# Layer 0's output product with 512 columns throughout, and its first feed-forward pair from the scaled residual stream

## Chip, cores and metric

One core of a Trainium2 chip runs the whole kernel in one launch. The metric is the device time of that launch in microseconds (us), taken as the median of repeated runs. The engines are named as in the profile: PE (TensorE, matrix products; PEld loads its stationary operand), DVE (VectorE), ACT (ScalarE), POOL (GpSimd) and SP (SyncE, which issues the DMAs).

## What is computed

Two layers of a diffusion trunk on 512 tokens of width 1024: 256 latent tokens x and 256 context tokens ctx, which go through the same weights with modulation values of their own. Layer 1 computes the latent tokens alone behind its attention. What matters here is the seam of layer 0 between the output product and the feed-forward network, for both halves of the tokens:

```python
def rms_norm(x, g):
    y = x * lax.rsqrt(jnp.mean(x * x, axis=-1, keepdims=True) + EPS)
    return y * g

m = ga * (ya @ w_br_a) + gb * (yb @ w_br_b) + gc * (yc @ w_br_c)
x = x + gx1 * (m @ w_out)                       # output product, 1024 x 1024
u2 = rms_norm(x, norm2_g) * (1 + cx2) + sx2     # scale cx2, shift sx2
x = x + gx2 * ((silu(u2 @ w_ff1) * (u2 @ w_ff3)) @ w_ff2)   # 1024 -> 2816 -> 1024
```

The modulation values (sx2, cx2 and the others) are six products of a conditioning vector with a 1024 x 6144 matrix in each layer; the ctx half has its own.

## The kernel before

**Products.** All data stand with the features on the 128 partitions and the tokens in the free dimension. Numbers are fp32. Weights and activations are split into a high and a low part, and each product is three matmuls (`mm3`, L227 to L229): high by high, high weight by low activation, low weight by high activation. A weight unit is 256 rows by 256 columns; one DMA on SP brings it as `raw`, one ACT copy makes its high part `wh` (L133) and one DVE subtraction its low part `wl` (L145). Both work ahead of PE by a few units; seven `raw` buffers stand ready, so that the next DMA waits for the `wl` that frees one. Results are accumulated in four PSUM banks (`acc`), two for each pair of 128 output columns.

**The stretch.** `into_job` makes 256 output columns of `w_out` in a job; jp counts the four jobs. `into` sets up jp 0 and 1 with all 512 tokens, then jp 2 and 3 for the x half with 256 tokens and again for the ctx half; the second run uses the weight parts of the first. For each 128 output columns DVE adds the product times a gate to the residual stream, once for each half (`xT`, L1135), and ACT and DVE square it and sum the squares (`ssq`, L530). At jp 3 of a half, `norm_rest` is put to the side work: one product with ones sums the squares over the partitions (`ss`, L543), ACT and DVE make the reciprocal root (`rstd`, `norm_rstd`), and `norm_u` goes over the eight blocks of 128 features: `ut` = x times scale times rstd (DVE, L571), `uh` = ut plus shift (ACT), `ul` = the rest (DVE, L580). The first feed-forward pair (`ff_job` with fp 0: 256 columns of `w_ff1` and 256 of `w_ff3`) then runs on the x half and, with the same weight parts, on the ctx half. The other ten pairs run with 512 tokens.

**What sets the order.** Each engine runs its instructions in the order in which the program puts them; a scheduler behind the program's text may move one a few places. The main loop goes over the jobs and after every few matmuls lets the side generators take a step. One generator, `mod_bg`, makes modulation groups in the background: for group j it loads eight pieces of 512 KB (`mraw`, two buffers, issued on SP among the `raw`), and for each piece and each half DVE multiplies and adds 1024 columns (`macc`, L489 and L491); then come two transposes (L496), two reduces (L497), a small product (L501) and four additions into `mod` (L505). In this stretch group 8 (shift and scale of the feed-forward norm) ends and group 10 runs. `hold`, set at jp 3 with the norm and cleared at the end of `norm_u`, stops this generator.

**Layer 1** runs its own first pair already in another way (`ff_first`, L1302 to L1304): the operand is x times the scale, split into `xh` (ACT) and `xl` (DVE, L1283) by `scaled_u`, with the shift as two more columns of `xh` (so 258 columns). The norm and the shift are put in behind the products: `ff` = product times rstd (L1310), `b` = the sum of the two shift columns (L1312), then silu with `b` as bias.

Of the kernel before, what the change touches and what calls it, by code (L numbers as in the profile page):

```python
# [8 lines left out]
F32 = mybir.dt.float32  # L9
# [5 lines left out]
P = 128  # L15
D = 1024
KT = D // P
SEQ = 256
# [156 lines left out]
class Trunk:  # L175
    def __init__(self, ctx, tc, a, out):
        self.nc, self.tc, self.a, self.out = tc.nc, tc, a, out
        self.cp = ctx.enter_context(tc.tile_pool(name="cp", bufs=1))
        self.gp = ctx.enter_context(tc.tile_pool(name="gp", bufs=61))
# [12 lines left out]
        self.xr = []  # L192
        self.keep = deque()
        self.plain = {}
# [337 lines left out]
    def norm_open(self, l, which):  # L532
        self.r0 = self.g([P, TOK], name="rstd")
        self.which = l, which
        last = self.which == (DEPTH - 1, 1)
        self.uu = [self.gT(SEQ, "u") if last else self.g2([P, TOK], "u") for _ in range(KT)]

    def norm_rstd(self, c):

# [19 lines left out]
    def norm_u(self, kts, vs):  # L559

        nc = self.nc
        l, which = self.which
        todo = [(kt, slice(v * SEQ, (v + 1) * SEQ), v) for kt in kts for v in vs]
        ts = {}

        def normed(i):
            if i < len(todo):
                kt, c, v = todo[i]
                ts[i] = self.g([P, SEQ], name="ut")
                g = self.A[l][which][:, kt, v : v + 1]  # L570
# [4 lines left out]
        for i, (kt, c, v) in enumerate(todo):  # L575
            hi, lo = (t[:, c] for t in self.uu[kt])
# [646 lines left out]
    def into_job(self, l, name, g0, which, sl, jp, k0=0, nkt=KT, more=False):  # L1223

        w = self.a[name][l]
        norm = jp == 3 and not more
        plain = which == 0 and l == DEPTH - 1

        def run(get):
            rhs = self.m if which == 0 else self.h[k0 : k0 + nkt]  # L1230
# [36 lines left out]

    def split_shift(self, l):

        t = self.sp.tile([P, KT, 2], F32R, tag="sh", bufs=1, name="shift")  # L1270
        sh = self.mod[l][:, 24 : 24 + KT, 0]
        self.split(t[:, :, 0], t[:, :, 1], sh)
# [12 lines left out]

    def ff_first(self, l):


        def run(get):
            nc = self.nc  # L1290
            mm = nc.tensor.matmul
            res = []
            for i in range(2):
                ps = [self.acc(), self.acc()]
                for u in range(KT // 2):
                    hi, lo = get(256)
                    for c in range(2):
                        cs = slice(c * P, (c + 1) * P)
                        for k in range(2):
                            kt = 2 * u + k  # L1300
                            xh, xl = self.plain[kt]
                            mm(ps[c][:, : SEQ + 2], hi[:, k, cs], xh, start=kt == 0, stop=False)  # L1302
                            mm(ps[c][:, :SEQ], hi[:, k, cs], xl, start=False, stop=False)
                            mm(ps[c][:, : SEQ + 2], lo[:, k, cs], xh, start=False, stop=kt == KT - 1)  # L1304
                        yield
                self.side.until(lambda: "rstd" in self.done)
                for c in range(2):
                    b = self.small(1, "b")
                    t = self.g([P, SEQ], name="ff")
                    nc.vector.tensor_tensor(t, ps[c][:, :SEQ], self.r0[:, :SEQ], ALU.mult)  # L1310
                    nc.scalar.activation(b, ps[c][:, SEQ : SEQ + 1], AF.Copy)
                    nc.vector.tensor_tensor(b, b, ps[c][:, SEQ + 1 : SEQ + 2], ALU.add)  # L1312
                    if i == 0:
                        nc.scalar.activation(t, t, AF.Silu, bias=b)
                        res.append(t)
                        continue
                    nc.vector.scalar_tensor_tensor(t, t, b, res[c], ALU.add, ALU.mult)
                    h = self.gT(SEQ, "h")
                    self.split(h[0], h[1], t)
                    self.h.append(h)  # L1320

        return self.units(self.a["w_ff1"][l], 0) + self.units(self.a["w_ff3"][l], 0), run

    def norm_rest(self, sl, ends):
        yield NORM_C if sl.start else NORM_X
        self.norm_rstd(sl)
        if self.which == (DEPTH - 1, 1):
            self.done.add("rstd")
# [127 lines left out]
    def program(self):  # L1456
        jobs = []
        self.bg_jobs = [(0, j, 2) for j in range(4, 12, 2)] + [(1, j, 2 if j < 4 else 1) for j in range(0, 12, 2)]
        for l in range(DEPTH):
# [17 lines left out]
            whole = slice(0, T)  # L1477
            parts = [slice(v * SEQ, (v + 1) * SEQ) for v in range(T // SEQ)]

            def into(*args):  # L1480

                res = [self.into_job(*args[:4], whole, jp, *args[4:]) for jp in range(2)]
                return res + [self.into_job(*args[:4], sl, jp, *args[4:]) for sl in parts for jp in range(2, 4)]

            jobs += into(l, "w_out", 16, 0)
            for f0, f1 in ((0, FT),) if last else ((0, FFA), (FFA, FT)):
                for fp in range(f0 // 2, f1 // 2):
                    if fp == 0 and last:
                        jobs.append(self.ff_first(l))
                        continue  # L1490
                    jobs += [self.ff_job(l, sl, fp) for sl in (parts if fp == 0 else [whole])]
                if last:
                    need = {("mod", l, 10), ("mod", l, 11)}

# [7 lines left out]
                elif f1 < FT:  # L1502
                    jobs += [self.into_job(l, "w_ff2", 40, 1, whole, jp, f0, f1 - f0, True) for jp in range(4)]
                else:
                    jobs += into(l, "w_ff2", 40, 1, f0, f1 - f0)
        return jobs

    def run(self):
# [75 lines left out]
```

## Time and profile before

| | before |
|---|---|
| time, median of 3 runs | 1229.56 us (1229.47 to 1229.62) |
| profiled execution | 1229.05 us, its span 1227.2 us |
| PE busy | 1196.7 us (98%) |
| DVE busy | 928.7 us (76%) |
| ACT busy | 643.2 us (52%) |
| DMA, mean over the span | 151 GB/s |

Times in rows are microseconds from the start of the span. A duration is longer than the distance to the next start where instructions overlap in an engine's pipeline, so costs are taken from starts. A tile's name is that of the program without its number, and L1135 is line 1135 of the kernel. A row's bracket gives the time for which the engine was idle before it, and what it waited for.

### The profile page before, as it was taken

Reading aid. Unit: us, or ns where it says so; the run is one execution under the profiler, and the core shown is the slowest. Engines: PE = TensorE matmul, PEld = TensorE weight load, DVE = VectorE, ACT = ScalarE, POOL = GpSimd, SP = SyncE. Lnnn points to the kernel's source line nnn. Section 1 sums busy time; section 2 is a strip of 40 time slices with the busy share of each in tenths; the row PEclk is TensorE's granted clock in tenths of the full one; section 3 lists DMA queues with packets and bytes.
Section 4 is the critical chain, followed back from the end, with each engine's and each line's share of the span. In section 5 each row is a group of like instructions: output and inputs, shape, how many; then the busy total and the mean of one; then the engine's idle time right before and its main releaser. Section 6 shows DMA issues by size and latency. Waiting matters only on the chain.

```text
span 1227.2 us, 20247 instructions
## 1 busy us (share of the span) xinstructions
PE 1196.7 (98%) x7059; PEld 1059.1 (86%) x7059; DVE 928.7 (76%) x1744; ACT 643.2 (52%) x1393; POOL 136.6 (11%) x185
## 2 busy tenths in 40 slices
PE   7899999999999999999999999998999999999998
PEld 2788889788888988888888888998999999999987
DVE  5867789989898996768566764778889778765554
ACT  4755587666434543332223333456878667655642
POOL 3243410101100000000000000154012100000000
PEclk9899999999999999999999999999999999999999
DMA  8722244334464535455666663243244565666563
GB/s 288 217 78 76 76 134 123 98 104 158 129 207 144 173 104 180 154 165 162 197 201 195 206 203 114 79 126 92 83 115 115 154 195 167 197 183 182 162 194 114
DMA packets 157522, 185.44 MB, mean 151 GB/s; under 512 B 12792, under 2 KB 135532, under 8 KB 157420
## 3 DMA queue, kind: packets, MB, share of 16 engines
q1 hardware_dynamic: 155612, 181.49, 47.6%
q0 software_dynamic: 1808, 2.66, 1.9%
q8 instruction: 55, 0.90, 0.3%
q14 instruction: 47, 0.39, 0.1%
HBM read 183.05 MB, written 1.05 MB: 150 GB/s over the span
## 4 chain that ended last, share of the span: by engine, by line
PE 80%; DVE 6%; DMA 5%; ACT 3%; POOL 3%; issue 2%; SPq 1%; DVEq 0%; ACTq 0%; POOLq 0%
PE acc L227 24%; PE acc L228 24%; PE acc L229 24%; DMA whole<-in_w_mod_dram 2%; PE y L842 2%; DMA raw<-in_w_in_dram 1%; DVE wl L145 1%; PE pt L888 1%; PE s L865 1%; POOL rs L686 1%; ACT wh L133 1%; PE s L866 1%; DVE macc L491 1%; ACT p L831 1%; DMA mraw<-in_w_mod_dram 1%
## 5 line engine op out<-in xcount | busy, mean ns | idle before, releaser
L133 ACT ACTIVATE wh<-raw 128x512 fp32r<-128x512 f32 (+2 forms) x512 | 307.9, 613 | 361.3 <-PE acc L228 229.7
L145 DVE TENSOR_TENSOR wl<-raw,wh 128x512 fp32r<-128x512 f32 (+2 forms) x512 | 343.3, 679 | 151.4 <-ACT wh L133 148.0
L227 PE MATMUL acc<-uh,wh 128*128 128x512 f32 (+1 forms) x784 | 279.8, 358 | 2.1 <-DVE v L239 1.0
L229 PE MATMUL acc<-uh,wl 128*128 128x512 f32 (+1 forms) x784 | 277.4, 355 | 2.4 <-DVE wl L145 2.4
L228 PE MATMUL acc<-ul,wh 128*128 128x512 f32 (+1 forms) x784 | 277.9, 355 | 0.2 <-DVE ul L580 0.2
L491 DVE SCALAR_TENSOR_TENSOR macc<-mraw,sf,macc 128x1024 f32<-128x1024 f32 x112 | 144.6, 1295 | 49.0 <-DMA mraw<-in_w_mod_dram 48.8
L229 PEld LDWEIGHTS acc<-uh,wl 128*128 128x128 f32 x784 | 148.9, 190 | 22.8 <-DVE wl L145 2.6
L227 PEld LDWEIGHTS acc<-uh,wh 128*128 128x128 f32 x784 | 148.7, 190 | 22.8 <-ACT gate L1100 1.8
L228 PEld LDWEIGHTS acc<-ul,wh 128*128 128x128 f32 x784 | 149.1, 190 | 19.9 <-DVE ul L580 0.4
L227 PE MATMUL acc<-wh,uh 128*128 128x384 f32 (+1 forms) x304 | 100.4, 331 | 4.6 <-ACT uh L1376 4.4
L228 PE MATMUL acc<-wl,uh 128*128 128x384 f32 (+1 forms) x304 | 98.8, 325 | 2.3 <-DVE wl L145 2.3
L229 PE MATMUL acc<-wh,ul 128*128 128x384 f32 (+1 forms) x304 | 99.0, 326 | 0.0
L227 PE MATMUL acc<-u,wh 128*128 128x256 f32 x320 | 91.4, 286 | 0.1
L229 PE MATMUL acc<-u,wl 128*128 128x256 f32 x320 | 91.0, 284 | 0.0
L228 PE MATMUL acc<-u,wh 128*128 128x256 f32 x320 | 90.5, 283 | 0.0
L227 PE MATMUL acc<-hh,wh 128*128 128x512 f32 (+1 forms) x216 | 75.9, 351 | 0.0
L229 PE MATMUL acc<-hh,wl 128*128 128x512 f32 (+1 forms) x216 | 75.6, 350 | 0.0
L228 PE MATMUL acc<-hl,wh 128*128 128x512 f32 (+1 forms) x216 | 75.5, 350 | 0.0
L227 PEld LDWEIGHTS acc<-wh,uh 128*128 128x128 f32 x304 | 59.2, 195 | 6.1 <-ACT uh L1376 4.5
L228 PEld LDWEIGHTS acc<-wl,uh 128*128 128x128 f32 x304 | 59.5, 196 | 3.5 <-DVE wl L145 2.6
L227 PEld LDWEIGHTS acc<-u,wh 128*128 128x128 f32 x320 | 61.4, 192 | 0.8 <-issue 0.5
L229 PEld LDWEIGHTS acc<-u,wl 128*128 128x128 f32 x320 | 61.4, 192 | 0.3 <-issue 0.2
(287 smaller groups left out, 2326.8 us busy)
## 6 DMA issues: line engine op xcount, KB each, us to landing
raw<-in_w_ff_dram SPq DMA_DIRECT2D x264, 256.0 KB, 3.0
mraw<-in_w_mod_dram SPq DMA_DIRECT2D x80, 512.0 KB, 4.0
raw<-in_w_in_dram SPq DMA_DIRECT2D x112, 256.0 KB, 2.9
raw<-in_w_in_dram SPq DMA_DIRECT2D x144, 64.0 KB, 2.0
whole<-in_w_mod_dram SPq DMA_DIRECT2D x32, 256.0 KB, 5.1
raw<-in_w_out_dram SPq DMA_DIRECT2D x32, 256.0 KB, 2.9
raw<-in_w_in_dram SPq DMA_DIRECT2D x16, 192.0 KB, 3.2
raw<-in_w_br_c_dram SPq DMA_DIRECT2D x8, 256.0 KB, 3.0
```

The source lines that it names most:

```text
L133: self.nc.scalar.activation(hi[:, :n], self.raw[i][:, :n], AF.Copy)
L145: self.nc.vector.tensor_tensor(lo[:, :n], self.raw[i][:, :n], self.hi[i][:, :n].bitcast(F32), ALU.subtract)
L227: mm(out, st[0], mv[0], start=start, stop=False)
L228: mm(out, st[0], mv[1], start=False, stop=False)
L229: mm(out, st[1], mv[0], start=False, stop=stop)
L491: nc.vector.scalar_tensor_tensor(acc[v], w, c, acc[v], ALU.mult, ALU.add)
L686: nc.gpsimd.tensor_tensor(rs, rs, self.mhalf[:, : 4 * nh], ALU.pow)
L831: nc.scalar.activation(pt, ps, AF.Exp, scale=-1.0, bias=m, accum_out=s[:, 0:1])
L842: mm(o, st, t[:, kt % 2, :], start=kt == 0 and i == 0, stop=kt == n - 1 and i == 1)
L865: nc.tensor.matmul(ps, st, ks[h][0], start=True, stop=False)
L866: nc.tensor.matmul(ps, st, ks[h][1], start=False, stop=True)
L888: nc.tensor.transpose(ps[:, kt * P : (kt + 1) * P], pr[h, qt][:, kt * P : (kt + 1) * P], self.ident)
```

## The change

Layer 0 runs all four jobs of `w_out` with 512 tokens (`into([whole], ...)`), and its first feed-forward pair becomes `ff_first`, which so far only layer 1 used. `ff_first` now takes the number of halves `nv` from the tokens: for `w_ff1` it runs the x half and then the ctx half with the same weight parts, and so for `w_ff3`. `scaled_u` splits x times scale for each half. So `plain` holds in both layers, and group 8 of the modulation must be done by jp 0 of `w_out`. `norm_rest` runs once for 512 tokens and tells with `("rstd", l)` that the evacuation may begin. `u` is still made for the pairs from 1 on; its tiles are taken one by one in `norm_u`, and the pool `gp` has 60 buffers of a slightly larger size where it had 61. Lines of the new code stand 1 to 10 higher (L1135 is L1136, L571 is L570, L580 is L581, L1283 is L1287, L1310 and L1312 are L1320 and L1322).

```diff
     def scaled_u(self, l, kt):
...
-        hi, lo = self.g([P, SEQ + 2], F32R, name="xh"), self.g([P, SEQ], F32R, name="xl")
-        x, g = self.xT[:, kt, 0:SEQ], self.A[l][1][:, kt, 0:1]
-        nc.scalar.activation(hi[:, :SEQ], x, AF.Copy, scale=g)
-        nc.scalar.activation(hi[:, SEQ:], self.shift[:, kt, :].bitcast(F32), AF.Copy)
-        nc.vector.scalar_tensor_tensor(lo, x, g, hi[:, :SEQ].bitcast(F32), ALU.mult, ALU.subtract)
+        nv = self.T // SEQ
+        hi = self.g([P, nv, SEQ + 2], F32R, name="xh")
+        lo = self.g([P, nv, SEQ], F32R, name="xl")
+        for v in range(nv):
+            x, g = self.xT[:, kt, v * SEQ : (v + 1) * SEQ], self.A[l][1][:, kt, v : v + 1]
+            nc.scalar.activation(hi[:, v, :SEQ], x, AF.Copy, scale=g)
+            nc.vector.scalar_tensor_tensor(lo[:, v, :], x, g, hi[:, v, :SEQ].bitcast(F32), ALU.mult, ALU.subtract)
+        nc.scalar.activation(hi[:, :, SEQ:], self.shift[:, kt, 0:nv, :].bitcast(F32), AF.Copy)
...
     def ff_first(self, l):
+        nv = self.tokens // SEQ
...
             for i in range(2):
-                ps = [self.acc(), self.acc()]
-                for u in range(KT // 2):
-                    hi, lo = get(256)
+                us = []
+                for v in range(nv):
+                    ps = [self.acc(), self.acc()]
+                    for u in range(KT // 2):
+                        if v == 0:
+                            us.append(get(256))
+                        hi, lo = us[u]
...
+                                mm(ps[c][:, : SEQ + 2], hi[:, k, cs], xh, start=kt == 0, stop=False)
+                                mm(ps[c][:, :SEQ], hi[:, k, cs], xl, start=False, stop=False)
+                                mm(ps[c][:, : SEQ + 2], lo[:, k, cs], xh, start=False, stop=kt == KT - 1)
+                            yield
+                    self.side.until(lambda: ("rstd", l) in self.done)
                     for c in range(2):
...
+                        nc.vector.tensor_tensor(t, ps[c][:, :SEQ], self.r0[:, v * SEQ : (v + 1) * SEQ], ALU.mult)
+                        nc.scalar.activation(b, ps[c][:, SEQ : SEQ + 1], AF.Copy)
+                        nc.vector.tensor_tensor(b, b, ps[c][:, SEQ + 1 : SEQ + 2], ALU.add)
...
-            jobs += into(l, "w_out", 16, 0)
+            jobs += into([whole], l, "w_out", 16, 0)
             for f0, f1 in ((0, FT),) if last else ((0, FFA), (FFA, FT)):
                 for fp in range(f0 // 2, f1 // 2):
-                    if fp == 0 and last:
-                        jobs.append(self.ff_first(l))
-                        continue
-                    jobs += [self.ff_job(l, sl, fp) for sl in (parts if fp == 0 else [whole])]
+                    jobs.append(self.ff_job(l, whole, fp) if fp else self.ff_first(l))
```

**How the order moves.** The rows below are instructions in the order in which an engine runs them, with the program's numbers on the tiles; they carry no times.

DVE at the end of the first output job. `acc_715` and `acc_716` are its accumulators, `mraw0_10_k` piece k of group 10. Before:

```order
L242 SCALAR_TENSOR_TENSOR ml_714_4493<-mix_712_4489,mh_713_4492 128x512
L145 TENSOR_TENSOR wl147_4552<-raw147_4405,wh147_4538 128x512
L1135 SCALAR_TENSOR_TENSOR xT_83<-acc_715_4496,mod0_110,xT_83 128x256 x2
L1135 SCALAR_TENSOR_TENSOR xT_83<-acc_716_4497,mod0_110,xT_83 128x256 x2
L505 TENSOR_TENSOR mod0_110<-modt_719_4578,cols0_109 32x16 x4
L145 TENSOR_TENSOR wl_724_4592<-raw148_4427,wh_717_4556 128x512
L530 TENSOR_TENSOR ssq_84<-ssq_84,sq_718_4575 128x512
L520 SCALAR_TENSOR_TENSOR A01_112<-mod0_110,cols0_109 128x16
L145 TENSOR_TENSOR wl_726_4611<-raw149_4454,wh_725_4596 128x512
L491 SCALAR_TENSOR_TENSOR macc_720_4585<-mraw0_10_1_4587,sf_105,macc_720_4585 128x1024
```

The same place after:

```order
L491 SCALAR_TENSOR_TENSOR macc_719_4506<-mraw0_10_1_4507,sf_105,macc_719_4506 128x1024
L242 SCALAR_TENSOR_TENSOR ml_714_4493<-mix_712_4489,mh_713_4492 128x512
L145 TENSOR_TENSOR wl147_4572<-raw147_4405,wh147_4557 128x512
L491 SCALAR_TENSOR_TENSOR macc_718_4505<-mraw0_10_2_4550,sf_105,macc_718_4505 128x1024
L1136 SCALAR_TENSOR_TENSOR xT_83<-acc_715_4496,mod0_110,xT_83 128x256 x2
L145 TENSOR_TENSOR wl148_4617<-raw148_4427,wh148_4576 128x512
L1287 SCALAR_TENSOR_TENSOR xl_721_4588<-xT_83,A01_112,xh_720_4587 128x256
L1136 SCALAR_TENSOR_TENSOR xT_83<-acc_716_4497,mod0_110,xT_83 128x256
L1287 SCALAR_TENSOR_TENSOR xl_721_4588<-xT_83,A01_112,xh_720_4587 128x256
L1136 SCALAR_TENSOR_TENSOR xT_83<-acc_716_4497,mod0_110,xT_83 128x256
L491 SCALAR_TENSOR_TENSOR macc_719_4506<-mraw0_10_2_4550,sf_105,macc_719_4506 128x1024
```

The four additions L505 and the gain L520, which stood behind the first residuals, now stand ahead of them (with `mix_709` and `mix_712`, just above these rows); three `macc` have come ahead too, and each residual is followed by an `xl`.

DVE at the norm. Before, in the norm of the ctx half; `wl_811` is the low part of the last unit of `w_ff3`, and `acc_814` and `acc_815` belong to the first pair:

```order
L580 SCALAR_TENSOR_TENSOR ul_760_4857<-ut_807_5091,mod0_110,uh_759_4856 128x256
L571 SCALAR_TENSOR_TENSOR ut_810_5106<-xT_83,A01_112,rstd_758_4855 128x256
L580 SCALAR_TENSOR_TENSOR ul_762_4859<-ut_808_5093,mod0_110,uh_761_4858 128x256
L145 TENSOR_TENSOR wl_811_5109<-raw163_4777,wh_803_5074 128x512
L571 SCALAR_TENSOR_TENSOR ut_812_5123<-xT_83,A01_112,rstd_758_4855 128x256
L580 SCALAR_TENSOR_TENSOR ul_764_4861<-ut_809_5096,mod0_110,uh_763_4860 128x256
L580 SCALAR_TENSOR_TENSOR ul_766_4863<-ut_810_5106,mod0_110,uh_765_4862 128x256
L491 SCALAR_TENSOR_TENSOR macc_720_4585<-mraw0_10_6_5234,sf_105,macc_720_4585 128x1024
L571 SCALAR_TENSOR_TENSOR ut_813_5134<-xT_83,A01_112,rstd_758_4855 128x256
L571 SCALAR_TENSOR_TENSOR ut_816_5152<-xT_83,A01_112,rstd_758_4855 128x256
L580 SCALAR_TENSOR_TENSOR ul_768_4865<-ut_812_5123,mod0_110,uh_767_4864 128x256
```

After, in the norm of both halves; `acc_761` and `acc_762` are the accumulators of the group w1 by x half, `acc_785` and `acc_786` those of w1 by ctx half:

```order
L581 SCALAR_TENSOR_TENSOR ul_780_5021<-ut_776_4995,mod0_110,uh_779_5020 128x256
L570 SCALAR_TENSOR_TENSOR ut_782_5033<-xT_83,A01_112,rstd_758_4926 128x256
L581 SCALAR_TENSOR_TENSOR ul_780_5021<-ut_777_5005,mod0_110,uh_779_5020 128x256
L1320 TENSOR_TENSOR ff_759_4927<-acc_761_4929,rstd_758_4926 128x256
L1320 TENSOR_TENSOR ff_760_4928<-acc_762_4930,rstd_758_4926 128x256
L570 SCALAR_TENSOR_TENSOR ut_789_5057<-xT_83,A01_112,rstd_758_4926 128x256
L1322 TENSOR_TENSOR b_783_5036<-b_783_5036,acc_761_4929 128x1
L581 SCALAR_TENSOR_TENSOR ul_788_5055<-ut_781_5023,mod0_110,uh_787_5054 128x256
L1322 TENSOR_TENSOR b_784_5041<-b_784_5041,acc_762_4930 128x1
L570 SCALAR_TENSOR_TENSOR ut_790_5067<-xT_83,A01_112,rstd_758_4926 128x256
L581 SCALAR_TENSOR_TENSOR ul_788_5055<-ut_782_5033,mod0_110,uh_787_5054 128x256
L1320 TENSOR_TENSOR ff_759_4927<-acc_785_5046,rstd_758_4926 128x256
```

Before, the low part of the last unit and the second norm stood here, and four `macc` of group 10 after. Now `ut` and `ul` of both halves, a transpose and a reduce of group 10 (just above and below these rows) stand around the evacuation of the first pair.

PE at the first pair. Before, the products of the ctx half with `w_ff3` read the normalised `uh` and `ul`:

```order
L227 MATMUL acc_815_5138<-uh_767_4864,wh_801_5056 128x256
L228 MATMUL acc_815_5138<-ul_768_4865,wh_801_5056 128x256
L229 MATMUL acc_815_5138<-uh_767_4864,wl_802_5070 128x256
L227 MATMUL acc_815_5138<-uh_769_4866,wh_801_5056 128x256
L228 MATMUL acc_815_5138<-ul_770_4867,wh_801_5056 128x256
L229 MATMUL acc_815_5138<-uh_769_4866,wl_802_5070 128x256
```

After, where the third group (w3 by x half, `acc_805`) follows the second (w1 by ctx half, `acc_786`):

```order
L1312 MATMUL acc_786_5047<-xh_756_4918,wh_749_4870 128x258
L1313 MATMUL acc_786_5047<-xl_757_4919,wh_749_4870 128x256
L1314 MATMUL acc_786_5047<-xh_756_4918,wl_750_4884 128x258
L1312 MATMUL acc_805_5146<-xh_720_4587,wh_751_4888 128x258
L1313 MATMUL acc_805_5146<-xl_721_4588,wh_751_4888 128x256
L1314 MATMUL acc_805_5146<-xh_720_4587,wl_763_4931 128x258
L1312 MATMUL acc_805_5146<-xh_723_4604,wh_751_4888 128x258
```

The operands are now `xh` and `xl`, and `acc_805` uses the PSUM bank that `acc_761` had, `acc_806` that of `acc_762`, and the fourth group (`acc_821`, `acc_822`) those of `acc_785` and `acc_786`. Pair 1 follows with the banks of the third group.

## Rows read from the trace of the kernel before

**Rows 1.** The page: busy time (us, share, instructions) of PE; the chain by engine.
```profile
PE 1196.7 (98%) x7059; PEld 1059.1 (86%) x7059; DVE 928.7 (76%) x1744; ACT 643.2 (52%) x1393; POOL 136.6 (11%) x185
...
PE 80%; DVE 6%; DMA 5%; ACT 3%; POOL 3%; issue 2%; SPq 1%; DVEq 0%; ACTq 0%; POOLq 0%
```

**Rows 2.** Timeline of PE: start us, duration, line, tiles, [idle before <-releaser].
```profile
380.79 0.39 PE L227 MATMUL acc<-mh,wh 128*128 128x512 f32 x1
...
402.79 0.28 PE L227 MATMUL acc<-mh,wh 128*128 128x256 f32 x1
...
441.07 0.38 PE L229 MATMUL acc<-uh,wl 128*128 128x256 f32 x1 [2.41 <-DVE wl L145]
...
442.52 0.41 PE L229 MATMUL acc<-uh,wl 128*128 128x256 f32 x1
...
444.65 0.34 PE L227 MATMUL acc<-uh,wh 128*128 128x256 f32 x1
...
445.54 0.28 PE L228 MATMUL acc<-ul,wh 128*128 128x256 f32 x1
...
455.14 0.40 PE L227 MATMUL acc<-uh,wh 128*128 128x512 f32 x1
```

**Rows 3.** Slices: us, busy PE, PEld, DVE, ACT, POOL, then clock, DMA share, GB/s.
```profile
400.00:413.00 13.00, 13.00 (x100) 12.49 (x99) 12.76 (x19) 6.02 (x11) 0.00 (x0) 1.00 0.62 197
413.00:426.00 13.00, 13.00 (x107) 12.74 (x106) 12.75 (x24) 7.57 (x16) 0.00 (x0) 1.00 0.55 168
426.00:440.00 14.00, 12.51 (x96) 11.71 (x94) 13.70 (x34) 8.45 (x20) 0.00 (x0) 1.00 0.40 118
440.00:455.00 15.00, 13.93 (x103) 13.93 (x104) 13.78 (x24) 5.78 (x12) 0.00 (x0) 0.89 0.35 119
455.00:470.00 15.00, 15.00 (x70) 12.47 (x69) 8.39 (x13) 4.97 (x9) 0.00 (x0) 1.00 0.34 106
```

**Rows 4.** Timeline of DVE from the start of the output product.
```profile
380.34 0.68 DVE L1115 SCALAR_TENSOR_TENSOR mix<-gate,acc 128x512 f32<-128x512 f32 x1
380.93 0.68 DVE L145 TENSOR_TENSOR wl<-raw,wh 128x512 fp32r<-128x512 f32 x1
...
390.51 0.88 DVE L1135 SCALAR_TENSOR_TENSOR xT<-acc,mod,xT 128x256 f32<-128x256 f32 x2 [2.59 <-PE acc L229]
...
392.67 0.71 DVE L505 TENSOR_TENSOR mod<-modt,cols 32x16 f32<-32x16 f32 x4
...
399.69 2.48 DVE L491 SCALAR_TENSOR_TENSOR macc<-mraw,sf,macc 128x1024 f32<-128x1024 f32 x2 [0.70 <-DMA mraw<-in_w_mod_dram]
402.19 1.68 DVE L1135 SCALAR_TENSOR_TENSOR xT<-acc,mod,xT 128x256 f32<-128x256 f32 x4
...
440.33 0.69 DVE L145 TENSOR_TENSOR wl<-raw,wh 128x512 fp32r<-128x512 f32 x1
```

**Rows 5.** Timeline of PE in layer 1's first pair; 29 steps lie between.
```profile
1031.78 0.28 PE L1302 MATMUL acc<-xh,wh 128*128 128x258 f32 x1
...
1035.27 0.28 PE L1304 MATMUL acc<-xh,wl 128*128 128x258 f32 x1
```

**Rows 6.** Timeline of DVE behind the first pair: a transpose.
```profile
451.01 1.24 DVE L496 STREAM_TRANSPOSE mtr<-macc 128x1024 f32<-128x1024 f32 x1
```

**Rows 7.** Timeline of DVE in layer 1: evacuation of the first pair.
```profile
1042.43 0.75 DVE L1310 TENSOR_TENSOR ff<-acc,rstd 128x256 f32<-128x256 f32 x2
```

**Rows 8.** What DVE waited for from 380 to 426 us: total, times, longest.
```profile
DVE xT L1135 <- PE acc L229: 3.1, 2, 2.6
DVE macc L491 <- DMA mraw<-in_w_mod_dram: 0.9, 2, 0.7
DVE ml L242 <- ACT mh L237: 0.7, 1, 0.7
DVE wl L145 <- ACT wh L133: 0.6, 2, 0.3
```

**Rows 9.** The page: a DMA issue's KB and us to landing.
```profile
mraw<-in_w_mod_dram SPq DMA_DIRECT2D x80, 512.0 KB, 4.0
```

More of the change, by code (lines that the diff above doesn't have):

```diff
@@ L178, in __init__ @@
         self.cp = ctx.enter_context(tc.tile_pool(name="cp", bufs=1))
-        self.gp = ctx.enter_context(tc.tile_pool(name="gp", bufs=61))
+        self.gp = ctx.enter_context(tc.tile_pool(name="gp", bufs=60))
         self.wp = ctx.enter_context(tc.tile_pool(name="wp", bufs=4))
@@ L534, in norm_open @@
         self.which = l, which
-        last = self.which == (DEPTH - 1, 1)
-        self.uu = [self.gT(SEQ, "u") if last else self.g2([P, TOK], "u") for _ in range(KT)]
+        self.uu = [None if l or which else self.g2([P, TOK], "u") for _ in range(KT)]
     def norm_rstd(self, c):
@@ L575, in norm_u @@
         for i, (kt, c, v) in enumerate(todo):
+            if self.uu[kt] is None:
+                self.uu[kt] = self.gT(SEQ, "u") if self.which == (DEPTH - 1, 1) else self.g2([P, TOK], "u")
             hi, lo = (t[:, c] for t in self.uu[kt])
@@ L1226, in into_job @@
         norm = jp == 3 and not more
-        plain = which == 0 and l == DEPTH - 1
+        plain = which == 0
         def run(get):
@@ L1268, in split_shift @@
     def split_shift(self, l):
-        t = self.sp.tile([P, KT, 2], F32R, tag="sh", bufs=1, name="shift")
-        sh = self.mod[l][:, 24 : 24 + KT, 0]
-        self.split(t[:, :, 0], t[:, :, 1], sh)
+        nv = self.T // SEQ
+        t = self.sp.tile([P, KT, 2, 2], F32R, tag="sh", bufs=1, name="shift")
+        sh = self.mod[l][:, 24 : 24 + KT, 0:nv]
+        self.split(t[:, :, 0:nv, 0], t[:, :, 0:nv, 1], sh)
         self.flush()
@@ L1278, in scaled_u @@
         nc = self.nc
[L1279 to L1283 removed]
+        nv = self.T // SEQ
+        hi = self.g([P, nv, SEQ + 2], F32R, name="xh")
[5 more added lines that the diff above has]
+        nc.scalar.activation(hi[:, :, SEQ:], self.shift[:, kt, 0:nv, :].bitcast(F32), AF.Copy)
         self.plain[kt] = hi, lo
     def ff_first(self, l):
+        nv = self.tokens // SEQ
         def run(get):
@@ L1291, in run @@
             mm = nc.tensor.matmul
-            res = []
+            res = [self.g([P, nv, SEQ], name="ff") for _ in range(2)]
             for i in range(2):
-                ps = [self.acc(), self.acc()]
-                for u in range(KT // 2):
-                    hi, lo = get(256)
-                    for c in range(2):
[L1298 to L1315, printed above, removed]
-                        continue
[L1317 to L1320, printed above, removed]
@@ L1322, in ff_first @@
-        return self.units(self.a["w_ff1"][l], 0) + self.units(self.a["w_ff3"][l], 0), run
+                us = []
[5 more added lines that the diff above has]
+                        hi, lo = us[u]
+                        for c in range(2):
+                            cs = slice(c * P, (c + 1) * P)
+                            for k in range(2):
+                                kt = 2 * u + k
+                                xh, xl = (x[:, v, :] for x in self.plain[kt])
+                                mm(ps[c][:, : SEQ + 2], hi[:, k, cs], xh, start=kt == 0, stop=False)
[3 more added lines that the diff above has]
+                    self.side.until(lambda: ("rstd", l) in self.done)
+                    for c in range(2):
+                        b = self.small(1, "b")
+                        t = res[c][:, v, :] if i == 0 else self.g([P, SEQ], name="ff")
+                        nc.vector.tensor_tensor(t, ps[c][:, :SEQ], self.r0[:, v * SEQ : (v + 1) * SEQ], ALU.mult)
+                        nc.scalar.activation(b, ps[c][:, SEQ : SEQ + 1], AF.Copy)
+                        nc.vector.tensor_tensor(b, b, ps[c][:, SEQ + 1 : SEQ + 2], ALU.add)
+                        if i == 0:
+                            nc.scalar.activation(t, t, AF.Silu, bias=b)
+                            continue
+                        nc.vector.scalar_tensor_tensor(t, t, b, res[c][:, v, :], ALU.add, ALU.mult)
+                        if v == 0:
+                            self.h.append(self.gT(self.T, "h"))
+                        self.split(*(x[:, v * SEQ : (v + 1) * SEQ] for x in self.h[c]), t)
@@ L1324, in norm_rest @@
+        keep = ("keep",) if nv > 1 else ()
+        return [u + keep for u in self.units(self.a["w_ff1"][l], 0) + self.units(self.a["w_ff3"][l], 0)], run
     def norm_rest(self, sl, ends):
@@ L1326, in norm_rest @@
         self.norm_rstd(sl)
-        if self.which == (DEPTH - 1, 1):
-            self.done.add("rstd")
+        if self.which[1]:
+            self.done.add(("rstd", self.which[0]))
         vs = range(sl.start // SEQ, sl.stop // SEQ)
@@ L1504, in program @@
                 else:
-                    jobs += into(l, "w_ff2", 40, 1, f0, f1 - f0)
+                    jobs += into(parts, l, "w_ff2", 40, 1, f0, f1 - f0)
         return jobs
```

3 lines of the change are left out of this document (1 added, 2 removed).

## Prediction

> **What bounds the kernel now.** I read the totals first: PE is busy for 98% of the span and carries 80% of the chain that ended last [rows 1]. By that alone any PE time saved would be time saved. The change, however, sits in one stretch, from the first matmul of layer 0's output product at 380.79 to the first full-width feed-forward matmul of column pair 1 at 455.14 [rows 2], 74.35 us. So I read that stretch by slices [rows 3]: from 400 on VectorE (DVE, the third of the busy figures) is busy for 12.76 of 13, 12.75 of 13, 13.70 of 14 and 13.78 of 15 us, while PE loses time only in the last two slices. Here two engines are full together, and PE is barely ahead. Where PE does lose time it loses it to DVE: 2.41 us before 441.07, waiting for a `wl` of L145 [rows 2, 4].
>
> What PE has to do there: a matmul with 512 columns takes 0.227 us from start to start (380.79 to 402.79 is 96 of them and a small one), one with 256 takes 0.12 (80 from 445.54 to 455.14) [rows 2]. So 96 x 0.227 + 384 x 0.12 + about 0.9 for the sums of squares = 68.8 us; the other 5.6 are the 2.41, a stretch at half clock behind it (10 matmuls from 442.52 to 444.65 at 0.213 instead of 0.12, about 17 in all, so 1.6 us) and small gaps [rows 2].
>
> **What the change takes from PE.** Of the output product 192 matmuls of 256 become 96 of 512: 23.0 to 21.8 us. The first pair's 192 stay at 256 or 258 columns; layer 1 runs that form already at 3.49 us for 29 steps, 0.120 each [rows 5]. New PE work: 192 x 0.227 + 192 x 0.120 + 0.9 = 67.5 us, and 0.3 for the small products, 67.8. Had PE nothing to wait for, pair 1 would start at 380.79 + 67.8 = 448.6, 6.5 us before 455.14: 1.2 of narrow matmuls and 5.3 of present loss, because the products no longer wait for normalised values.
>
> **What it puts on DVE.** Per 256 columns of each of 16 blocks there is one `xl` (L1287 of the new code): 16 x 0.40 = 6.3 us, at the pitch of the residual's four in a row (1.68 us for four of 0.48, so 0.40 each) [rows 4]. The 16 `ut` and 16 `ul` of the norm stay, since the pairs from 1 on still read normalised values. The evacuation of the first pair gains sixteen instructions, eight of them with one column, and the sums of squares lose some: small. More important is order. In the old code the norm of the x half set `hold` before the background product of modulation group 10 was done; its last four `macc` (0_10_6, 0_10_7) stood behind the whole norm, under the easy slice that follows. The new code sets `hold` only at the last of the four blocks, so all 14 `macc` still open, and their two transposes, now stand before or within the norm. And PE now needs two things of DVE that come late in that order. There are four accumulators; the third group of the first pair (w3, x half) takes the banks that the first group (w1, x half) gives back when `b_784` is added, and the fourth (w3, ctx half) those that `b_804` gives back.
>
> So the time is a sum over DVE's queue. Start at `mix_709<-gate` (380.34 [rows 4]), which stands at the same point in both orders, and count to the end of `b_784`: 110 instructions. 40 with 512 columns (24 of them `wl`) x 0.60 (380.34 to 380.93 [rows 4]) = 24.0; 14 `macc` x 1.20 (two in 2.48, of which the second lasts 1.28 [rows 4]) = 16.8; 16 residuals and 16 `xl` x 0.395 = 12.6; 7 `ut` and 5 `ul` = 4.7; two transposes and a reduce of 1024 at about 1.15 (a transpose lasts 1.24, less the 0.08 by which neighbours overlap [rows 4, 6]) = 3.5; two evacuations x 0.335 (0.75 for two of 0.42 [rows 7]) = 0.7; modulation adds (four in 0.71 [rows 4]) and the smallest rows = 1.0. Sum 63.3: **not before 443.6**, even if DVE never idles. PE, by its own work, reaches that point at 380.79 + 43.5 + 11.5 + 0.9 + 0.3 = 437.0.
>
> How much idle comes on top? The same sum over the old order, 102 instructions from the same start to the `wl` at 440.33, is 53.8 against 60.6 passed [rows 4, 6], 6.8 of idle: 3.1 for PE, 0.9 for transfers, 0.7 and 0.6 for ScalarE [rows 8], the rest gaps. The 3.1 goes: those residuals waited from 387.9 to 390.51 [rows 4], and now three `macc` and the four adds, 4.4 us, stand ahead of them. ScalarE's 1.3 and the gaps of 1.5 I leave. Transfers: the loads of 0_10_4 and 0_10_6 are queued on SP behind `raw156` and `raw160`, which wait for a `wl` five or six rows before the `macc` that reads them: 4.0 us of flight [rows 9], after the issue of the `raw` ahead, against 4.2 to 4.4 us of DVE work between, so about 0.5 each. Some of these waits will cover others. I take 2.5, from bounds of 0 (nothing but the queue) and 5 (all of the old idle but PE's, with both transfers as long again).
>
> - w3 x half starts at 443.6 + 2.5 = 446.1, some nine us after PE could have.
> - From `b_784` to `b_804` are 7.5 us of DVE work (fourteen `ut` and `ul`, a reduce, two evacuations, two `b`). That gives 453.6. The third group's 5.8 us on PE, and 1.6 more if the clock falls as it did after 441.07, lie inside it.
> - w3 ctx half 453.6 + 5.8 = 459.4. Pair 1 takes the banks that `b_817` frees, 5.4 us after `b_804` (six `ut` and `ul`, two `wl`, four adds of group 10, two evacuations with their `b` and one product), 459.0, so it isn't late again. Its start: 459.5, **4.4 us later than 455.14**; I add 0.3 for restarts of PE.
>
> Nothing is given back after: in 455 to 470 PE is busy for 15.00 of 15 with DVE at 8.39 [rows 3]; that the `macc` are done earlier only empties a slice that was not full. The profiled run (1229.05, span 1227.2) becomes 1233.8; against the median of 1229.56 the same +4.7 gives **1234.3**.
>
> **A rule against the row.** DVE is full in four slices in a row and PE is not [rows 3]. The Trainium skill (Perfetto Trace Analysis, "Identifying the Most-Contended Engine" and "Optimization Strategy") says to improve the engine with the highest occupancy, with the reservation that the most-contended engine may change between regimes. By the first half the PE work removed would come off the time: 448.6 for pair 1 and 1223 in all, the first rival below; the second half is what the slices show.
>
> **The rivals.**
>
> *PE sets the end (faster, 1223.1).* DVE reaches `b_784` before PE does, since the products wait for no normalised values: pair 1 at 448.6, 6.5 us earlier. For it: totals [rows 1], and layer 1, where the same form ran without a wait [rows 5]. Against it: layer 1 has 256 tokens, so half the `xl`, `ut` and `ul`, and no `macc` in between; the 63.3 us of work ahead of `b_784` would have to be 54.
>
> *DVE's queue without idle (no change, 1231.5).* If idle is 0, w3 x half starts at 443.6, w3 ctx half at 451.1 and pair 1 at 457.0 with the restarts: +1.9. For it: slices with 12.76 of 13 [rows 3]. Against it: 1.3 us of waits for ScalarE that the change doesn't remove [rows 8], and more work on ScalarE (16 `xh`).
>
> *Longer waits and a second fall of the clock (slower, 1238).* Idle of 5 gives 448.6, 456.1 for w3 ctx half; if PE then runs that group's first part at half clock, as it did from 441.07 to 444.65 after 2.41 us of waiting (steps of 0.213, the 1.2 GHz level; granted clock 0.89 over the slice [rows 2, 3]), 1.6 more: 456.1 + 5.8 + 1.6 = 463.5, +8.4. It decides if PE waits in the fourth group as it does in the third. Beside the row: the Trainium skill (TensorE: Matmul & The Clock Gate, "A second HAM failure mode: psum-queue depth-cycling") describes a kernel where small waits between groups that cycle through PSUM banks made the clock go up and down; by that rule both of my waits would be followed by such a stretch, as in this rival.
>
> *The change is not what it says.* Not so: the order shows 96 matmuls fewer, 512 columns in all four blocks, and the first pair ahead of the norm's values. No chance is kept for it.
>
> **How the numbers follow.** Forecast, 1232.2 to 1236.5, with 0.54; no idle 0.15; longer waits 0.21; PE sets the end 0.10. About 0.2%, 2.5 us, is what a measurement of this kernel can tell from no change. The case without idle lies inside it (the limit is 1232.0), with a little of the forecast's tail: same 0.17. The first rival alone is faster, 0.10, and the rest is slower, 0.73. The range leaves out the first rival and the tail of the third: 1230.0 to 1239.0.
>
> **What would show it.** Right: in the changed profile PE waits for a `b` of L1322 before the third group of the first pair, for 5 to 10 us, DVE has no idle slice from 388 to 459, and pair 1 starts near 459.5. `xl` rows of 0.48 us and a first matmul of 512 columns where there were 256 show the two parts. Wrong: PE busy throughout, or waiting for a `wl` or for `xh` of ScalarE instead; `macc` waiting for transfers by more than 2 us in sum; `b_784` before 442.

## The result: 0.85% slower, by two causes of which one was forecast

| | before | changed |
|---|---|---|
| time, median | 1229.59 us (4 runs) | 1240.21 us (1238.23 to 1240.45, 4 runs) |
| span of the profiled execution | 1227.2 us | 1238.5 us |
| output product starts [rows 2] | 380.79 | 385.04 |
| pair 1 starts [rows 2] | 455.14 | 463.49 |
| the stretch between them | 74.35 us | 78.45 us |
| pair 1 to the end of the span | 772.1 us | 775.0 us |

The ratio is 1.0085 (95% interval 1.0073 to 1.0096): 10.6 us more, where 4.7 were forecast and 1239.0 was the upper end of the range. The stretch lost 4.1 us, close to what was forecast. The other 7.2 us of the span lie outside it, 4.25 before and 2.9 behind, where the change does little but alter the pool's buffer size. From here on "stretch" means the time from the first matmul of the output product to the first of pair 1.

Timeline of PE in the changed kernel: the start of the output product, the seam between the second and third group of the first pair, the fourth group, pair 1.

```profile
385.04 0.48 PE L227 MATMUL acc<-mh,wh 128*128 128x512 f32 x1
...
441.88 0.28 PE L1314 MATMUL acc<-xh,wl 128*128 128x258 f32 x1
449.76 0.58 PE L1312 MATMUL acc<-xh,wh 128*128 128x258 f32 x1 [7.60 <-DVE b L1322]
450.14 0.41 PE L1313 MATMUL acc<-xl,wh 128*128 128x256 f32 x1
450.35 0.42 PE L1314 MATMUL acc<-xh,wl 128*128 128x258 f32 x1
...
457.71 0.36 PE L1312 MATMUL acc<-xh,wh 128*128 128x258 f32 x1
...
463.49 0.40 PE L227 MATMUL acc<-uh,wh 128*128 128x512 f32 x1
```

PE waits once, 7.6 us, and for the `b` of L1322 as forecast; it starts again behind the first of the two `b`, `b_783` (row 449.56 below), since the first six matmuls of the third group need its bank alone. Then it runs at half clock (steps of 0.21). The slices, with the columns of [rows 3], show DVE nearly full all the way (93 to 99% of each slice) and PE at 7.40 of 15 us from 440 to 455:

```profile
400.00:413.00 13.00, 13.00 (x58) 10.52 (x57) 12.89 (x22) 6.40 (x15) 0.00 (x0) 1.00 0.50 163
413.00:426.00 13.00, 13.00 (x58) 10.53 (x57) 12.67 (x20) 6.51 (x14) 0.00 (x0) 1.00 0.45 142
426.00:440.00 14.00, 14.00 (x99) 12.84 (x98) 13.44 (x23) 8.74 (x20) 0.00 (x0) 1.00 0.54 157
440.00:455.00 15.00, 7.40 (x47) 7.20 (x46) 14.52 (x32) 8.27 (x20) 0.00 (x0) 0.77 0.29 99
455.00:470.00 15.00, 15.00 (x102) 13.76 (x101) 13.89 (x41) 7.14 (x18) 0.00 (x0) 1.00 0.18 54
```

DVE's rows at the ends of the forecast sums: `mix_709`, then `b_783` and `b_784`, then the second pair of `b`:

```profile
384.83 0.68 DVE L1116 SCALAR_TENSOR_TENSOR mix<-gate,acc 128x512 f32<-128x512 f32 x1
...
449.56 0.14 DVE L1322 TENSOR_TENSOR b<-b,acc 128x1 f32<-128x1 f32 x1
...
450.02 0.15 DVE L1322 TENSOR_TENSOR b<-b,acc 128x1 f32<-128x1 f32 x1
...
457.42 0.21 DVE L1322 TENSOR_TENSOR b<-b,acc 128x1 f32<-128x1 f32 x2
```

**Outside the stretch.** Laid beside each other, the two traces drift apart evenly where PE does nothing but 512-column matmuls: 8.35 us at pair 1, 14.9 at 767 us of the old kernel. In layer 1, with 256 columns, they come together again to about 10. Two rows six steps apart show the pace, the time from one start to the next. Changed kernel, 1.39 us for six:

```profile
499.64 0.39 PE L227 MATMUL acc<-uh,wh 128*128 128x512 f32 x1
...
501.03 0.40 PE L227 MATMUL acc<-uh,wh 128*128 128x512 f32 x1
```

Kernel before, 1.36 us for six:

```profile
500.28 0.39 PE L227 MATMUL acc<-uh,wh 128*128 128x512 f32 x1
...
501.64 0.39 PE L227 MATMUL acc<-uh,wh 128*128 128x512 f32 x1
```

Over 1158 and 1197 neighbouring starts from 500 to 800 us the means are 0.2267 and 0.2317. PE waits for nothing there in either kernel, and nothing of the change runs there. What differs is where tiles lie in memory: `xh` with 2 x 258 columns made every buffer of `gp` 2064 bytes wide. In the compiled program's addresses a buffer now takes 2080, so that the pool's tiles start at all multiples of 32, while most weight parts, which lie in a pool behind it, start at remainder 224 of 256; before, all activations and all weight parts that the wide matmuls read started at one remainder of 256 bytes, 96.

### The profile page after: what moved, and what is told of

Same layout as the page of the kernel before. It is cut to its first block, busy times and chain, and to the rows that moved or that the text cites. A ratio compares the mean times of both kernels' runs of the same rounds, so it can differ in the third digit from the quotient of the medians.

```text
span 1238.5 us, 20122 instructions
## 1 busy us (share of the span) xinstructions
PE 1203.7 (97%) x6961; PEld 1049.8 (85%) x6961; DVE 937.2 (76%) x1770; ACT 650.1 (52%) x1419; POOL 137.2 (11%) x185
## 5 line engine op out<-in xcount | busy, mean ns | idle before, releaser
L227 PE MATMUL acc<-uh,wh 128*128 128x512 f32 (+1 forms) x720 | 263.4, 366 | 2.2 <-DVE v L239 1.0
L228 PE MATMUL acc<-ul,wh 128*128 128x512 f32 (+1 forms) x720 | 261.1, 363 | 0.0
L229 PE MATMUL acc<-uh,wl 128*128 128x512 f32 (+1 forms) x720 | 260.7, 362 | 0.0
L227 PEld LDWEIGHTS acc<-uh,wh 128*128 128x128 f32 x720 | 135.6, 188 | 25.0 <-ACT gate L1101 1.8
L229 PEld LDWEIGHTS acc<-uh,wl 128*128 128x128 f32 x720 | 135.7, 189 | 22.2
L228 PEld LDWEIGHTS acc<-ul,wh 128*128 128x128 f32 x720 | 135.7, 188 | 21.5
```

The source lines that it names most:

```text
L227: mm(out, st[0], mv[0], start=start, stop=False)
L228: mm(out, st[0], mv[1], start=False, stop=False)
L229: mm(out, st[1], mv[0], start=False, stop=stop)
```

## Experiments on the pace

These run the kernel before, with the same instructions in the same order (with 2304 bytes some rows around the attention stand otherwise, since the pool has only 54 buffers), and move tiles alone. Each comparison is with runs of the kernel before on the same chip (medians 1228.1 to 1228.8). First the width of a buffer, by taking each tile of `g` as a part of a wider one (here 516 numbers, 2064 bytes):

```diff
-        return self.gp.tile(shape, dt, tag="g", name=self.nm(name))
+        t = self.gp.tile([P, 516], dt, tag="g", name=self.nm(name))[:, :n]
```

> The kernel before with one thing of the changed kernel: each of the gp pool's buffers is 2064 bytes per partition instead of 2048 (60 buffers, as in the changed kernel); instructions and their order are those of before. Theory A (pace): the matmuls with 512 columns go at 0.232 us instead of 0.227 because the tiles no longer lie at multiples of 2048 bytes. Then this kernel takes about 1235 to 1237 us, its 512-column matmuls in 500 to 800 us step at 0.232, and the 256-column ones of layer 1 at 0.119. Theory B (the slower pace comes with the change's own work, its traffic on DVE, ACT and DMA): 1229.6 within 0.2%, steps of 0.227.

Measured: 1238.04 us, ratio 1.0076 (1.0061 to 1.0091); steps of 0.2321 from 500 to 800 us, 0.1182 for 256 columns. So the buffer width alone costs 9.3 us, with no other part of the change: theory A, by more than I had expected. (One buffer less, 60 for 61, is no cause: the run with 64 bytes below has 60 too, and the old pace.)

> The kernel before with buffers of 2112 bytes (a multiple of 64, not of 2048; 59 buffers), same instructions and order. Theory A1 (what costs is that tiles start off a multiple of 64 bytes): 1229.6 within 0.2%, steps of 0.227. Theory A2 (what costs is any distance other than 2048): 1235 to 1237, as with 2064. Theory B: 1229.6.

Measured: 1235.81, ratio 1.0055 (1.0040 to 1.0070), steps of 0.2313. A multiple of 64 does not help.

> The kernel before with buffers of 2304 bytes (a multiple of 256, not of 2048; 54 buffers). If a tile's start off a multiple of 256 bytes is what slows 512-column matmuls: steps of 0.227 and 1230 to 1232 (as the control with 53). If only 2048 is free of it: steps of 0.231 to 0.232 and 1236 to 1239.

Measured: 1229.35, ratio 1.0010 (0.9999 to 1.0021), steps of 0.2267. A distance other than 2048 is harmless, if it keeps all tiles at one remainder of 256: A2 falls. Then only unused bytes were put ahead of the pool (as here) or behind it, with 60 buffers of 2048 bytes:

```diff
+        self.pad = ctx.enter_context(tc.tile_pool(name="pad", bufs=1))
+        self.pad.tile([P, 16], F32, tag="pad", name="pad")
```

> The kernel before with 64 unused bytes ahead of gp (60 buffers of 2048 bytes): every tile of gp and the weight parts behind it start 64 bytes higher, all still at one remainder of 256 (160 instead of 96). Instructions and order as before. If the pace hangs on the distance of tiles from each other: 0.227 and 1229 within 0.2%. If on an absolute place in 256 bytes: 0.231 to 0.232 and 1235 to 1238.

Measured: 1229.17, ratio 1.0005 (0.9993 to 1.0017), steps of 0.2269. The absolute place doesn't matter.

> The kernel before with 64 unused bytes behind gp: the activations stay at remainder 96 of 256, the weight parts, which lie behind, go to 160. Order as before. If what counts is that weights (stationary) and activations (moving) have one remainder: 0.231 to 0.232 and 1235 to 1238. If what counts is the distance of the activations' tiles among themselves: 0.227 and 1229.

Measured: 1237.84, ratio 1.0068 (1.0047 to 1.0089), steps of 0.2333. The activations kept their distances and the pace was lost: what counts is the weights' place against the activations'. Contention with the vector and scalar engines does not explain it: over the 213 steps from 500 to 800 us during which neither DVE nor ACT worked the mean is 0.2332.

> The kernel before with 128 unused bytes behind gp: weight parts at remainder 224 of 256, activations at 96. If the step is 64 or 128: 0.227 and 1229. If the step is 256: 0.231 to 0.234 and 1234 to 1239.

Measured: 1238.63, ratio 1.0086 (1.0071 to 1.0101), steps of 0.2327.

> The kernel before with 256 unused bytes behind gp: weight parts and activations again at one remainder of 256 (96). If the step is 256: 0.227 and 1229 within 0.2%. If it is larger (512 to 2048): 0.231 to 0.234 and 1234 to 1239.

Measured: 1229.08, ratio 1.0003 (0.9988 to 1.0018), steps of 0.2267. So the pace returns with a whole 256. The slices from 500 to 560 us, PE full in both, say the same by the number of matmuls. 64 bytes off:

```profile
500.00:560.00 60.00, 60.00 (x260) 48.35 (x259) 41.94 (x56) 18.82 (x31) 0.00 (x0) 1.00 0.49 154
```

256 bytes off:

```profile
500.00:560.00 60.00, 60.00 (x267) 49.71 (x267) 44.80 (x59) 20.52 (x34) 0.00 (x0) 1.00 0.49 155
```

**One pair or the whole stream?** The kernels with mixed remainders hold many matmuls whose own weights and activation do share a remainder. From 500 to 800 us these are hardly faster than the rest: with 2112 bytes 312 such steps have a mean of 0.2303 against 0.2313 for all, in the changed kernel 182 have 0.2316 against 0.2317. Where twelve of them follow each other, the pace comes back on the way. In the run with 2112 bytes six steps take 1.39 us and the next six 1.35; by the compiled program's addresses all twelve read at remainder 32:

```profile
1209.64 0.39 PE L234 MATMUL acc<-wh,h 128*128 128x512 f32 x1
...
1211.03 0.39 PE L234 MATMUL acc<-wh,h 128*128 128x512 f32 x1
...
1212.38 0.39 PE L234 MATMUL acc<-wh,h 128*128 128x512 f32 x1
```

The five other such places in the two kernels with 2112 bytes have the same mean step, 0.2293 to 0.2295. So the pace belongs to a run of matmuls and not to a single one.

## Experiments on the stretch

**The change without the slow pace.** The changed kernel with buffers of 2304 bytes:

> The changed kernel with buffers of 2304 bytes (54), at which the kernel before kept 0.227 and took 1229.35. So the change without the slower pace: the stretch at 78.4 against 74.4 to 74.9, no drift elsewhere: 1229.35 + 3.5 to 4 = about 1233. If the change had a second cost outside the stretch: 1235 or more.

Measured: 1232.68, ratio 1.0033 (1.0022 to 1.0044); stretch 78.95 against 74.87 in the run of the kernel before with the same buffers, every later section equal within 0.3 us; the output product starts 0.8 us later than there. So the change by itself costs about 3 us (1232.68 less 1229.35 is 3.3, by the ratios 2.8), and the rest of the 10.6, some 7, goes with the pace. The 9.3 of the buffer width alone and these 3 do not add up to 10.6; why the slow pace costs less in the changed kernel is not shown. With 2112 bytes, where the pace is slow:

> The changed kernel with buffers of 2112 bytes (59 buffers), same instructions and order as the changed kernel. If A1 holds, only the stretch of the output product is slower than before: 1229.6 + 4.4 = 1234, with pair 1 starting about 4 us later than 455.14 and no drift behind it. If A2 or B holds: 1240.

Measured: 1237.84, ratio 1.0072 (1.0056 to 1.0089); pace 0.2317, so A1 falls here too; stretch 78.03, 2.6 more than with the same buffers in the kernel before.

**One part alone.** In the kernel before, only the output product got 512 columns in all four blocks (`[whole]` for `w_out`). "Theory D" in the next texts says that DVE's queue ahead of the evacuation sets the end of the stretch.

> One part of the change alone, in the kernel before (2048-byte buffers, 61 of them): the output product with 512 columns in all four blocks; the norm once for both halves; the first feed-forward pair as before, on normalised values. PE's own work falls by 1.2 us, but the first pair must now wait for the whole chain residual, sum of squares, rstd, ut, uh, ul behind the last output block. Theory D: PE waits there 6 to 12 us (half clock behind it), so 1233 to 1240. Rival (the background macc hide nothing and the chain is as short as for one half): 1229 to 1231.

Measured: 1236.55, ratio 1.0069 (1.0048 to 1.0089), stretch 83.01. What PE waited for in it:

```profile
PE ss L543 <- DVE ssq L530: 5.5, 1, 5.5
PE acc L227 <- ACT uh L578: 5.3, 1, 5.3
```

Here PE waits 5.5 and 5.3 us. The wide product puts the whole chain of the norm behind it; the other half of the change, products that don't need the norm, takes 4.1 us of this loss back (83.0 to 78.95).

**Is it DVE's queue?** The background products stopped from the first output job on, with 2112 bytes:

```diff
                 if plain:
                     self.split_shift(l)
+                if plain and l == 0:
+                    self.hold = True
```

> The changed kernel with buffers of 2112 bytes, and the background products of modulation group 10 stopped from the first output job to the end of the norm: 12 of the 14 macc and the two transposes move behind the first pair. Theory D (DVE's queue ahead of the evacuation sets the end of the stretch): 12 x 1.20 + 3.5 = 17.9 us leave the queue before b_784; its sum falls to 45, PE waits for the norm's own chain instead, by 2 to 4 us, and pair 1 starts 5 to 8 us earlier than in the run with 2112 and without this edit: time 6.5 below that run, so about 1227.5 if that gives 1234. Rival (PE waits for rstd and its chain, not for DVE's queue): within 2 us of that run.

Measured: 1236.01, 1.8 us below the run without the edit, which is the rival's mark (within 2 us) and not theory D's 6.5; stretch 75.27, 2.8 us less, PE's wait 4.6 instead of 7.3. The traces say which part of the queue counted. The slices from 395 to 425 us, without and with the edit, show PE full in both and DVE idle for 12 us where the `macc` are gone:

```profile
395.00:425.00 30.00, 30.00 (x131) 24.41 (x130) 29.32 (x45) 15.18 (x33) 0.00 (x0) 1.00 0.45 148
395.00:425.00 30.00, 30.00 (x131) 24.40 (x131) 17.86 (x35) 15.13 (x33) 0.00 (x0) 1.00 0.30 80
```

The first residual of the last output block, without and with it:

```profile
425.26 0.48 DVE L1143 SCALAR_TENSOR_TENSOR xT<-acc,mod,xT 128x256 f32<-128x256 f32 x1
425.74 0.88 DVE L1143 SCALAR_TENSOR_TENSOR xT<-acc,mod,xT 128x256 f32<-128x256 f32 x2 [1.92 <-PE acc L236]
```

The output product started at 381.99 and 382.47, so this row stands 43.27 us behind it in both: PE's own work sets it, and the twelve `macc` ahead of it (14.4 us of DVE) cost nothing there. The gain lies behind it: from this row to the end of the first `b` 21.0 us became 18.2, about the two transposes and the reduce (3.5 us) that stood among the norm's rows. What is left ahead of `b` is the norm's chain with 7 `ut` and 4 `ul`. For the next runs `xh` got a pool of its own, which leaves `gp` at 2048 bytes, but only with 53 buffers:

```diff
-        hi = self.g([P, nv, SEQ + 2], F32R, name="xh")
+        hi = self.xp.tile([P, nv, SEQ + 2], F32R, tag="xh", name=self.nm("xh"))
```

> Control for the next three: the kernel before with 53 buffers of 2048 bytes in gp (instead of 61) and 14 instead of 16 in the small pool, which moves some hundred instructions around the attention of layer 0 and nothing in the stretch. 1229 within 0.2% (2.5 us), 512-column matmuls at 0.227.

Measured: 1231.61, ratio 1.0020 (1.0009 to 1.0031), pace 0.2267, 2.8 us above the kernel before and so just outside what was expected. The moved instructions ahead of the stretch cost it: the output product starts at 383.50 instead of 380.79.

> The changed kernel with the xh tiles (2064 bytes) in a pool of their own, 8 buffers, so that gp keeps buffers of 2048 bytes (53). Theory A2 (the pace of 512-column matmuls depends on the buffers' distance): pace back at 0.227, no drift outside the stretch, and the time above the control is only what the stretch loses, 2.5 to 4.5 us: 1231.5 to 1233.5. Rival B (the slower pace belongs to the change's work): pace 0.232 and 1238 to 1240.

Measured: 1234.45, ratio 1.0048 (1.0030 to 1.0065), 2.8 above the control; pace 0.2267, stretch 78.41, wait for `b` 6.9.

> As the run before, and the background products of group 10 stopped from the first output job to the end of the norm. With 2112-byte buffers that moved pair 1 by 2.7 us within the stretch and the wait of PE from 7.3 to 4.6 us. So 2 to 3 us below the run before, 1229 to 1231.

Measured: 1233.08, 2 us above what was expected; stretch 75.05. The stretch gives 3.4 us, the time 1.4; the intervals are as wide as that. Here the first residual of the last block comes 1.7 us earlier, counted from the product's start (42.75 instead of 44.45), so in this pair the `macc` ahead of it cost up to that much; 0.8 of it is a wait of PE for `ml`.

> As the run before, and the norm's ut and ul put off by 14 steps of the main loop, so that DVE evacuates the first two groups of the first pair before them. Theory D (what PE waits for is b_784 and b_804 behind the norm's ut and ul in DVE's queue): PE's wait falls from 4.6 to 1 to 3 us and does not come back at pair 1; 2 to 4 us below the run before, about 1226 to 1228, faster than both kernels. Rival: the ut and ul put off make pair 1 wait for uh and ul instead, and the time stays at that of the run before.

The edit, beside the `hold` above, in `norm_rest` behind `norm_rstd`:

```diff
+        if self.which == (0, 1):
+            yield 14
         yield from self.norm_u(range(KT), vs)
```

Measured: 1227.67, ratio 0.9991 (0.9981 to 1.0002), stretch 68.32. PE no longer waits for a `b`. But the part that takes 237.9 us in the kernel before (564 to 802 us) takes 241.1 here: the background products come late, and PE waits for `wl` in the narrow blocks of `w_ff2`.

> The changed kernel with xh in its own pool and the norm's ut and ul put off by 14 steps, without stopping the background products. Theory D: 4.7 us of ut and ul leave the queue before b_784 and most of the 7.5 us between b_784 and b_804: the wait of PE falls from 6.9 to about 2 to 4 and pair 1 starts 4 to 6 us earlier, so 1229 to 1231. Rival (only the macc matter): within 1 us of 1234.5.

Measured: 1226.95, ratio 0.9992 (0.9979 to 1.0004), stretch 69.21, wait for `b` 0.9. A larger gain than expected, and without stopping anything: the order of evacuation and norm is the larger part.

> The kernel with xh in its own pool, background stopped during the output product and the norm, ut and ul put off by 14 steps, and one thing new: for 60 steps behind the norm the background generator takes a step each time instead of every second time, so that its products don't come late at the narrow blocks of the second w_ff2 part, where the run without this lost 3.2 us (564 to 802 us: 241.1 against 237.9). Expected: that stretch back at 238, the stretch of the output product at 68.3, so 3 us below 1227.7: 1224 to 1225.5. Rival: the products now fill DVE in 452 to 530 and PE waits there instead: no gain.

Measured: 1229.60, ratio 1.0015 (1.0004 to 1.0027). The rival came true: stretch 68.78, but the next section 113.0 instead of 109.3, where PE now waits for `wl` and for `mr`.

**Both causes mended.** Buffers of 2304 bytes, and `yield 14` without the `hold`:

> As the run before, with ut and ul of the norm put off by 14 steps of the main loop. With xh in its own pool that gave a stretch of 69.2 us instead of 78.4. Here the same: 9 us below the run before, about 1224, 0.4% faster than the kernel before. Rival (the stretch's gain is lost later): over 1227.

Measured: 1224.38 us, ratio 0.9965 (0.9954 to 0.9977): 0.35% faster than the kernel before, as expected, and 8.3 us below the run without the edit. Timeline of PE: start, the one wait that is left, pair 1, 69.0 us after the start:

```profile
381.83 0.48 PE L234 MATMUL acc<-mh,wh 128*128 128x512 f32 x1
...
439.29 0.39 PE L1319 MATMUL acc<-xh,wh 128*128 128x258 f32 x1 [1.40 <-DVE b L1329]
...
450.84 0.39 PE L234 MATMUL acc<-uh,wh 128*128 128x512 f32 x1
```

## Why the prediction was wrong, point by point

**PE's own work, 67.8 us: right** where nothing holds PE. The stretch was 68.3 and 69.0 us in the runs with the evacuation first.

**DVE's sum, 63.3 and 2.5 of idle: right in size, in part by luck.** From `mix_709` at 384.83 to the end of `b_784` at 450.17 it was 65.3. The 2.0 of idle were made otherwise than I listed: 0.9 for ScalarE's `rs`, 0.3 for PE, gaps; no transfer of `mraw` was waited for, where I had put 1.0. The wait of PE, 7.6, lies in the 5 to 10 named. But the queue from its start is not what held PE. The last block's first residual (428.48) stands 43.4 us behind the start of the product, where PE's own matmuls put it; DVE's queue came through at the same time, 0.1 us before, and in the kernels with 2112 bytes the row stood in the same place without twelve of the `macc`. That the two agree there is luck. What held PE is the queue behind that row, 21 us to `b_783`; that its order is the cause is shown by the evacuation runs, in which the same instructions in another order took the wait from 7.3 to 1.4. "DVE is full in four slices in a row and PE is not" also misreads [rows 3]: in the first two PE is full as well, 13.00 of 13.

**From `b_784` to `b_804` 7.5 us, then 5.8 for the fourth group: right,** 7.46 and 5.78. The half clock behind the wait was hidden in the 7.5: it made the third group last from 449.76 to 457.71, and `b_804` was done at 457.63. So PE did not wait again, and no second fall came: the third rival's mechanism did not occur. Stretch 78.45 against 79.0 by the sum.

**Rivals.** PE does not set the end in this order, though it nearly does with the evacuation ahead. The queue without idle did not occur either: its idle was 2.0, nearer to the 2.5.

**The step that failed** is the one that took every duration from the trace of before and made the sum in the stretch alone: "Nothing is given back after", and nothing lost either. The text of the change says that `gp` has 60 buffers of a slightly larger size, and the prediction gave that no term. Its price is about 7 us of the span in the trace (the pace of 512-column matmuls went from 0.2267 to 0.2317), and 9.3 us with the kernel before alone (wider buffers, nothing else). Where the pace was kept, the changed kernel took 1232.68, inside the forecast. The range was too narrow for the same reason: all its bounds were bounds of the stretch.

## What to carry to other kernels

A tile that widens a shared buffer moves all tiles of the pool and all pools behind it; compare the addresses of what the matrix products read, before and after, and treat a change there as a change to every product in the kernel. In a stretch where two engines are full, add up the instruction queue of the slower one up to each release that the other needs, and start the sum anew at each row that waits for the other engine: here the sum gave the stretch within 0.6 us, but work in its first two thirds could be taken out for nothing. What frees an accumulator belongs in the queue ahead of work that is needed later: moving 32 `ut` and `ul` by 14 steps was worth more (8.3 us) than the matmuls that the change saved (1.2 us by the forecast's sum).

## What the runs showed of the hardware

The start-to-start time of a stream of 512-column matmuls (fp32 in the form used here, 128 x 128 weights) depends on where the weight parts and the activations start: 0.2267 to 0.2269 us if all have the same remainder of 256 bytes (distances of 2048 and 2304 between tiles, shifts of 64 of everything or of 256 of the weights), 0.2327 and 0.2333 if the weights are off by 128 and 64, 0.2313 to 0.2321 with mixed remainders. In the mixed kernels a single matmul with matching remainders is hardly faster (0.2303 and 0.2316); in twelve in a row the second six were (1.35 us against 1.39). Matmuls with 256 columns go the other way, 0.1195 in the first case and 0.1167 to 0.1187 in the others (840 to 1000 us). Why is open: no run separates the reading of the activations from the loading of the next weights, and distances under 64 bytes were not tried alone.
